# Six more early places for weight chunks of a mixture of experts, and the last norm's vectors loaded late

## The chip, the cores and the metric

The kernel runs on one core of a Trainium2 chip. The metric is the device time of one execution in microseconds (us); three runs of the kernel before gave a median of 1350.39 us. One further execution was taken with the hardware profiler, and all rows below come from that one.

## The reference

Two transformer layers over 256 tokens of width 1024. Layer 0 is a latent attention with a dense feed-forward part, layer 1 a sparse attention with a mixture of eight experts. Only the end of layer 1 matters here:

```python
x = layer_norm(alpha * x + h, ln_mix_g[i], ln_mix_b[i])
logits = xt @ w_router;  top_val, top_idx = lax.top_k(logits, 2);  wts = softmax(top_val)
h = silu(xb @ w_gate[e]) * (xb @ w_up[e])          # 1024 x 3584 twice, for each of 8 experts
y[token] += (h @ w_down[e]) * weight               # 3584 x 1024
x = layer_norm(alpha * x + y, ln_ffn_g[i], ln_ffn_b[i])
```

The eight experts hold 8 x 3 x 1024 x 3584 numbers of 4 bytes, 352 MB, and each is read once.

## The kernel before

**Chunks and places.** The expert weights come from HBM in chunks of 1 MB (some of 0.75 MB), each loaded by SP into a *place*, a tile of 128 x 2048 numbers. There are gate chunks, up chunks and down chunks; this text writes mg(e, j, i), mu(e, j, i) and md(e, j, i) for chunk i of step j of the expert that is worked on as number e. Expert 0 has three steps (512, 2048 and 1024 columns of the 3584), the others two (2048 and 1536). While PE multiplies the gate and up chunks of one step, the down chunks of the step before are put in between: mg, half of md, mu, the other half of md.

**Two kinds of expert.** Experts 0, 2, 4, 6 and 7 are `PLAIN`: PE multiplies the raw chunk as f32 (line 1631), and the place is free when PE has read it. Experts 1, 3 and 5 are split: ACT writes a high part (line 128) and DVE the rest (line 131) into halves `whi` and `wlo` of a ring, and the place is free when both halves are split. The ring has five pairs of halves; one pair is given away as a place (`ring_n`, `given`), which leaves four.

**The order of places** is written by hand (lines 416 to 419): a list `first` for the 18 chunks that are loaded by calls of `pre` while the dense first step of expert 0 runs, then a list `then` that is gone through over and over. A chunk may be loaded as soon as the chunk that had its place before it has been used (`add`, `fetch`, `loads`; `used` calls `loads`). SP issues loads strictly in order, so a load that waits for its place holds those behind it.

```python
first = [["four"] * 2] * 4 + ["hh"] + ["raw"] * 5 + ["xe", "xTh", "xTl", "xna", "xe", "s2", "x3Tl", ["whi", "wlo"]]
then = ["raw"] * 5 + ["xTh", "xTl", "xna", "s2", "x3Tl", ["whi", "wlo"]]
seq = first + then * 2 + (then + ["x3Th"]) * 30
```

With `x3Th` the list has 12 places, so a chunk takes the place of the chunk that came 12 before it. The same four chunks of step 0 of expert 0 are loaded into `four` tiles and split as well.

**Other tiles.** `y` (line 1601) collects the sums of the experts; `scale` (line 1419) starts it as ALPHA times the normed x, two ACT instructions in the dense step. `lng` holds gain and bias of a norm, copied to all 128 partitions by `bc_load` (line 450), two loads on POOL's queue; the last norm's pair is loaded at line 1594, some 850 us before it is used. In `run` (line 1733) the list `fq` holds small thunks; `fill(1)` after each down chunk and `fill(2)` after each gate or up chunk run the next ones.

Of the kernel before, what the change touches and what calls it, by code (L numbers as in the profile page):

```python
# [26 lines left out]
def body(tc, a, out, tap=None, upto=9):  # L27
# [33 lines left out]
    def slot(pool_, tag, bufs=1):  # L61
        return lambda: pool_.tile([128, 2048], F32, tag=tag, bufs=bufs, name=nm("raw"))
# [50 lines left out]
    def ring_half(z, n, dt=F32R):  # L113
        return st.tile([128, 1024], dt, tag=f"{z}{n}", bufs=1, name=nm(z))
# [48 lines left out]
    places = {"raw": s_raw, "four": lambda: four()}  # L163
    for z in ("xna", "xnb", "lng", "xTh", "xTl"):
        places[z] = slot(xp, z)
    for z in ("hh", "s2", "x3Th", "x3Tl"):
        places[z] = lambda z=z: slot(ep, z)()
    places["xe"] = slot(xo, "xe", 2)
    for z in ("whi", "wlo"):
        places[z] = lambda z=z: ring_half(z, given[0], F32)  # L170

    def add(key, src, shape, uses, own=None, auto=True, where="raw", plain=False):

# [27 lines left out]
    def pump(n=1, later=False):  # L201

        for _ in range(n):
            if not halves:
                return
            c, i = halves[0]
            if c.raw is None or c.blocked or c.n > cur[0] + 5 and c.key[0][0] == "m" and len(c.key) > 3:
                return
            if c.own is None:
                if not free:  # L210
                    if ring[0][0].uses[ring[0][1]] > 0:
                        return
                    free.append(ring.popleft()[2])
                    if len(free) + len(ring) > ring_n[0]:
                        given.append(free.pop())
                        continue
                n_ = free.popleft()
                ring.append((c, i, n_))
            elif i == 0:
                c.own = c.own()  # L220
            halves.popleft()

            def done(c=c, i=i):
                c.whole[i] = True
                loads()
            c.parts[i] = split_half(c.raw, i, c.own, later, done, None if c.own else n_)
# [33 lines left out]
            return tuple(t[:, k % (na // 2), c0:nb if c1 is None else c1] for t in c.parts[i])  # L260
        return w

    ring_n, given = [HL], []
    auto = [True]

    def mm3(o, l, r, first, last):
# [146 lines left out]
        yield from (("md", *prev, i) for i in range(wd // 256 - 2))  # L413
        yield from (("md", *prev, i, "tail") for i in range(2))

    first = [["four"] * 2] * 4 + ["hh"] + ["raw"] * 5 + ["xe", "xTh", "xTl", "xna", "xe", "s2", "x3Tl", ["whi", "wlo"]]
    then = ["raw"] * 5 + ["xTh", "xTl", "xna", "s2", "x3Tl", ["whi", "wlo"]]
    keys = list(moe_keys())
    seq = first + then * 2 + (then + ["x3Th"]) * 30
    for n, key in enumerate(keys):  # L420
        where = seq[n]
        if n == len(keys) - 1 and not isinstance(where, list):
# [27 lines left out]
    def bc_load(g, b, p=None, tag="lng"):  # L450

        t = (p or xp).tile([128, 2, D], F32, tag=tag, bufs=1, name=nm("lng"))
        pool.dma_start(t[:, 0, :], g.partition_broadcast(128))
        pool.dma_start(t[:, 1, :], b.partition_broadcast(128))
        return t[:, 0, :], t[:, 1, :]
# [22 lines left out]
    def ln_sums():  # L478
        return xp.tile([128, 16], F32, tag="lnst", bufs=2, name=nm("lnst"))
# [848 lines left out]
    def pre(*ns):  # L1328
        for n in ns:
            fetch(chunks[keys[n]])  # L1330
# [85 lines left out]
        dve.reciprocal(cs[:, 1], cs[:, 0])  # L1416
        dve.tensor_tensor(coef, coef, cs[:, 1, :, None].to_broadcast([128, 2, 8]), op=ALU.mult)

    def scale(t):
        act.activation(y[:, t, :], x3[:, t, :], AF.Copy, scale=ALPHA)  # L1420

    cnt = choice[:, 4]
    pool.tensor_copy(choice[:, 5], iota[:, 0:8])
    ordered = ep.tile([128, 6, 8], F32, name="ordered")
# [161 lines left out]
    transpose_x(x3, x3T, 1, 0)  # L1586
    transpose_x(x3, x3T, 1, 1)
    pump(1)
    pre(13, 14)
    g_ln, b_ln = bc_load(a["ln_ffn_g"][1], a["ln_ffn_b"][1])  # L1590
    dense_u(0, 0)
    logits()
    dense_g(1, 0)
    y = ep.tile([128, 2, D], F32, tag="y", name="y")
    pre(15)
    pump(1)
    logits_T()
    choose()
    dense_g(1, 1)
    pump(1)  # L1600
    slots()
    weigh()
    G0, th = gather(0, 0)
    th[0]()
    dense_u(0, 1)
    scale(0)
    hidden(0)
    scale(1)
    dense_u(1, 0)
    pump(1)  # L1610
    dense_u(1, 1)
    hidden(1)
    pre(16)
    now(th[1:5])
    pump(1)
    hT0 = hid_G(G0)
    flush()
    while ring:
        c, i, n_ = ring.popleft()
        assert c.uses[i] == 0  # L1620
        free.append(n_)
    ring_n[0] -= 1
    given.append(free.pop())
    th[5]()
    pre(17)
    loads()
    auto[0] = True

# [42 lines left out]
    def hidden_tile():  # L1671
        return ep.tile([128, 2048], F32, tag="hh", bufs=1, name=nm("hh"))
# [49 lines left out]
    def scatter(e, oo, ohT, hf, t, sums=None):  # L1722
        c = slice(hf * 512, hf * 512 + 512)
        p = pT()
        pe.matmul(p, ohT[:, t, :], oo[hf][0], start=True, stop=False)
        pe.matmul(p, ohT[:, t, :], oo[hf][1], start=False, stop=True)
        dve.scalar_tensor_tensor(y[:, t, c], p, by[0][:, 2 + t, e:e + 1], y[:, t, c], op0=ALU.mult, op1=ALU.add,
                                 accum_out=sums[t][:, hf:hf + 1] if sums is not None else None)

    def run(todo, G, at, gen=(), end=None):  # L1730


        nxt, acc = None, None
        for n, (e, base) in enumerate(todo):
            ss = widths(e, gen)
            for j, (c0, wd) in enumerate(ss):
                if at is not None and at[:2] == (e, j):
                    continue
                last_j = j == len(ss) - 1
                final = last_j and n == len(todo) - 1  # L1740
                if last_j and not final:
                    nxt, th = gather(*todo[n + 1])
                    th[0]()
                g = gate_up("mg", e, j, G, gen)
                fill(99)
                if len(order) == 1:
                    arrange()
                hh = hidden_tile()
                for z, p in each_bank(hh, g):
                    act.activation(z, p, AF.Silu)  # L1750
                m = 0
                if at is not None:
                    if at[1] == 0:
                        acc = [pB(), pB()]
                    at = (*at[:4], acc, gen)
                    m = widths(at[0], gen)[at[1]][1] // 256
                    down(at, range((m + 1) // 2))
                if last_j and not final:
                    fq.extend(th[1:])
                u = gate_up("mu", e, j, G, gen)  # L1760
                fill(99)
                for z, p in each_bank(hh, u):
                    dve.tensor_tensor(z, z, p, op=ALU.mult)  # L1763
                hT, ths = hid_T(hh, wd, G["plain"])
                if final:
                    now(ths[:0])
                    down(at, range((m + 1) // 2, (m + 1) // 2 + 1))
                    now(ths)
                    down(at, range((m + 1) // 2 + 1, m))
                else:  # L1770
                    down(at, range((m + 1) // 2, m)) if at is not None else None
                    if at is not None and at[0] != e:
                        scatters(at)
                    fq.extend(ths)
                at = (e, j, G, hT)
            if nxt is not None:
                G = nxt
        at = (*at, acc, gen)
        m = wd // 256
        if end is not None:  # L1780
            down(at, range(m - 2))
            oo = []
            end(lambda hf: down_tail(at, hf), lambda hf: oo.append(outs(acc, hf)),
                lambda hf, t, sums: scatter(e, oo, G["ohT"], hf, t, sums))
            return
        down(at, range(m))
        scatters(at)
        fill(99)
# [4 lines left out]
        fq.extend([lambda hf=hf, t=t: scatter(e, oo, G["ohT"], hf, t) for hf in range(2) for t in range(2)])  # L1793

    sums = [ln_sums() for _ in range(2)]

    def n_square(t, hf, scr):
        ln_square(sums[t], y[:, t, :], hf, scr)

    def n_gain(t, hf, z):  # L1800
        ln_gain(sums[t], y[:, t, :], z[:, t, :], g_ln, hf)

    def n_out(t, hf, z):
        ln_out(sums[t], z[:, t, :], b_ln, hf)
        sp.dma_start(out[0, t * 128:(t + 1) * 128, H[hf]], z[:, t, H[hf]])

    def norm_rest(z):
# [32 lines left out]
    assert not halves and not fq and all(c.uses == [0, 0] for c in plan)  # L1840
    man.close()
    free.clear()
    free.extend(z for z in range(HL) if z not in given)
    over = nc.values_load(ordi[0:1, 16:17], min_val=0, max_val=256)  # L1844
    with tc.If(over > 0):
        for e in range(E):
            count = nc.values_load(ordi[0:1, e:e + 1], min_val=0, max_val=256)
            for base in (64, 192) if e in PLAIN else (128,):
                with tc.If(count > base):
                    G, th = gather(e, base, True)  # L1850
                    now(th)
                    run([(e, base)], G, None, ("gen",))
        scr, z = norm_tiles()
        for t in range(2):
            for hf in range(2):
                dve.tensor_reduce(sums[t][:, hf:hf + 1], y[:, t, H[hf]], axis=AX.X, op=ALU.add)
                n_square(t, hf, scr)
        ln_mean(sums[0])
        n_gain(0, 0, z)
        norm_rest(z)  # L1860
# [66 lines left out]
```

## Time and profile before

| | |
|---|---|
| median of three runs | 1350.39 us (1349.46 to 1351.86) |
| the profiled execution, its time | 1349.32 us |
| the profiled execution, its span | 1347.5 us |
| PE busy | 1300.5 us, 97% of the span |
| DVE, ACT, POOL busy | 729.6, 597.3, 42.3 us |
| mean granted TensorE clock | 0.991 |
| DMA | 430.56 MB, of it 421.03 MB on SP's queue |

The span runs from the first to the last instruction; the time is the device time of the whole execution. The page cuts the span into 40 slices and gives for each the busy tenths of every engine, the granted clock and what the DMA engines moved; windows give the same for any stretch. In a timeline a row merges neighbouring equal instructions; a matmul of f32 appears as two records, and a matmul's end in the profile is a model, so its start and the start of the next are the better measure. For DMA issues the last column is the time from issue to landing.

### The profile page before, as it was taken

What the parts mean: (1) busy time and instruction counts of PE and PEld (TensorE: products, weight loads), DVE (VectorE), ACT (ScalarE), POOL (GpSimd) and SP (SyncE); (2) the same over time, 40 slices, a digit from 0 to 9 for tenths busy, and PEclk for the clock granted to TensorE, in tenths of its full rate; (3) what the DMA queues carried; (4) which work ended last, traced back from release to release, by engine and by line L of the source; (5) the groups of instructions that cost most, each with busy time, mean ns of one, the idle gap of its engine ahead of it and who ended that gap; (6) DMA issues with size and microseconds to landing.
All of it is one profiled execution on the core that took longest, in us unless ns stands there. A gap on an engine that the chain in (4) does not pass through costs nothing. (4 is left out here: it accounts for less than half of the span.)

```text
span 1347.5 us, 19685 instructions
## 1 busy us (share of the span) xinstructions
PE 1300.5 (97%) x7397; PEld 925.1 (69%) x7397; DVE 729.6 (54%) x1208; ACT 597.3 (44%) x949; POOL 42.3 (3%) x57
## 2 busy tenths in 40 slices
PE   8998999999999999999999999999999999999884
PEld 7878999989988674367974567894457895543221
DVE  5856555567777761168863257883337875400103
ACT  5554444445577541056752156763126674200001
POOL 0002000002100120000000000000000000000000
PEclk9998999999999999999999999999999999999998
DMA  9635555569622477999999999999999999999994
GB/s 315 211 107 177 165 181 187 188 193 278 197 66 78 146 276 270 410 418 418 417 419 415 418 419 419 416 420 399 418 420 419 416 419 400 418 417 420 418 419 172
DMA packets 127944, 430.56 MB, mean 320 GB/s; under 512 B 12463, under 2 KB 64949, under 8 KB 99808
## 3 DMA queue, kind: packets, MB, share of 16 engines
q1 hardware_dynamic: 125264, 421.03, 80.9%
q0 software_dynamic: 2576, 8.18, 2.1%
q8 instruction: 60, 0.98, 0.3%
q14 instruction: 44, 0.36, 0.1%
HBM read 428.11 MB, written 1.07 MB: 318 GB/s over the span
## 5 line engine op out<-in xcount | busy, mean ns | idle before, releaser
L131 DVE TENSOR_TENSOR wlo<-raw,whi 128x1024 fp32r<-128x1024 f32 (+2 forms) x365 | 413.7, 1152 | 225.2 <-ACT whi L128 216.2
L128 ACT CAST whi<-raw 128x1024 fp32r<-128x1024 f32 (+3 forms) x367 | 360.0, 994 | 255.2 <-PE pa L1631 63.7
L1631 PE MATMUL pa<-raw,xe 128*64 128x512 f32 (+1 forms) x1112 | 238.8, 570 | 6.2 <-DMA raw<-in_moe_w_up_dram 6.2
L1631 PE MATMUL pa<-whi,xe 128*128 128x512 f32 (+3 forms) x820 | 240.2, 382 | 0.0
L1631 PEld LDWEIGHTS pa<-raw,xe 128*64 128x64 f32 x1112 | 74.4, 134 | 146.6 <-issue 119.1
L1631 PEld LDWEIGHTS pa<-whi,xe 128*128 128x128 f32 (+1 forms) x820 | 145.9, 185 | 30.5 <-issue 8.3
L1631 PE MATMUL pa<-wlo,xe 128*128 128x512 f32 (+3 forms) x436 | 153.2, 389 | 0.0
L1631 PE MATMUL pb<-raw,four 128*64 128x512 f32 x520 | 119.0, 596 | 8.4 <-DMA raw<-in_moe_w_down_dram 8.4
L1631 PE MATMUL pb<-whi,four 128*128 128x512 f32 (+1 forms) x356 | 116.5, 408 | 0.0
L1763 DVE TENSOR_TENSOR hh<-hh,pa 128x512 f32<-128x512 f32 (+1 forms) x43 | 25.0, 620 | 145.1 <-PE pa L1631 144.9
L1631 PEld LDWEIGHTS pb<-raw,four 128*64 128x64 f32 x520 | 35.8, 136 | 83.7 <-issue 65.2
L1631 PEld LDWEIGHTS pa<-wlo,xe 128*128 128x128 f32 (+1 forms) x436 | 75.9, 182 | 15.2 <-issue 5.2
L1631 PEld LDWEIGHTS pb<-whi,four 128*128 128x128 f32 (+1 forms) x356 | 65.8, 185 | 24.4 <-issue 7.6
L1631 PE MATMUL pb<-wlo,four 128*128 128x512 f32 (+1 forms) x188 | 75.2, 418 | 0.0
L269 PE MATMUL pa<-xTh,whi 128*128 128x256 f32 x216 | 67.6, 313 | 0.0
L271 PE MATMUL pa<-xTh,wlo 128*128 128x256 f32 x216 | 61.1, 283 | 0.3 <-DVE wlo L131 0.3
L270 PE MATMUL pa<-xTl,whi 128*128 128x256 f32 x216 | 61.2, 283 | 0.0
L1750 ACT ACTIVATE hh<-pa 128x512 f32<-128x512 f32 (+1 forms) x43 | 21.5, 547 | 73.8 <-PE pa L1631 73.8
L269 PE MATMUL pb<-xTh,whi 128*128 128x256 f32 x176 | 49.9, 284 | 0.0
L270 PE MATMUL pb<-xTl,whi 128*128 128x256 f32 x176 | 49.8, 283 | 0.0
L271 PE MATMUL pb<-xTh,wlo 128*128 128x256 f32 x176 | 49.8, 283 | 0.0
L1537 ACT COPY four<-pt 128x512 f32<-128x512 f32 x10 | 5.8, 584 | 90.8 <-PE pt L1531 90.8
(413 smaller groups left out, 1982.3 us busy)
## 6 DMA issues: line engine op xcount, KB each, us to landing
raw<-in_moe_w_down_dram SPq DMA_DIRECT2D x102, 1024.0 KB, 13.2
raw<-in_moe_w_gate_dram SPq DMA_DIRECT2D x63, 1024.0 KB, 11.4
raw<-in_moe_w_up_dram SPq DMA_DIRECT2D x62, 1024.0 KB, 13.7
raw<-in_moe_w_gate_dram SPq DMA_DIRECT2D x51, 768.0 KB, 13.2
raw<-in_moe_w_up_dram SPq DMA_DIRECT2D x51, 768.0 KB, 11.2
raw<-in_nsa_w_in_dram SPq DMA_DIRECT2D x23, 512.0 KB, 7.2
raw<-in_ffn_w_gate_dram SPq DMA_DIRECT2D x11, 1024.0 KB, 5.4
raw<-in_ffn_w_up_dram SPq DMA_DIRECT2D x11, 1024.0 KB, 5.3
```

The costliest lines, as they stand in the source:

```text
L128: act.copy(hi[:, :h], src)
L131: (pool if later == "pool" else dve).tensor_tensor(lo[:, :h], src, f(hi[:, :h]), op=ALU.subtract)
L269: pe.matmul(o, lh, rh, start=first, stop=False)
L270: pe.matmul(o, lh, rl, start=False, stop=False)
L271: pe.matmul(o, ll, rh, start=False, stop=last)
L1537: (dve.tensor_copy if c0 else act.copy)(z, p[:, :n * 128])
L1631: pe.matmul(o, l, r, start=first, stop=last, skip_group_check=True)
L1750: act.activation(z, p, AF.Silu)
L1763: dve.tensor_tensor(z, z, p, op=ALU.mult)
```

## The change

- The four chunks of `first` that were 15 to 17, and six more, get places: `lng`, `s2`, `y`, three pairs of ring halves, `x3Tl`, and two more pairs. So 24 chunks are loaded by `pre` where 18 were, and the load list that follows begins with chunk 24.
- `freed(n)` takes the ring halves of the dense step out of the ring as their last matmul is written, and makes each pair a place. After the dense step one pair stays a place (`R[0]`), and four are the ring, as before.
- `then` gains `lng`, which makes 13 places with `x3Th`. From the first chunk of expert 6 (E - 2) on, `lng` is left out of the list, which makes 12.
- `y` is made and scaled in step 2 of expert 0, behind its gate chunks.
- `bc_load` of the last norm is gone. `gains`, called in step 1 of expert 6 behind its gate chunks, loads gain and bias as 2 x 4 rows of 256 numbers into `few` on SP's queue; four thunks, each two f32 matmuls of 256 columns against a row of the identity and an ACT copy of 512 columns, spread them to 128 partitions.

```diff
-    for z in ("hh", "s2", "x3Th", "x3Tl"):
+    for z in ("hh", "y", "s2", "x3Th", "x3Tl"):
...
-        places[z] = lambda z=z: ring_half(z, given[0], F32)
+        for i in range(HL):
+            places[f"{z}{i}"] = lambda z=z, i=i: ring_half(z, rings[i], F32)
...
-    first = [["four"] * 2] * 4 + ["hh"] + ["raw"] * 5 + ["xe", "xTh", "xTl", "xna", "xe", "s2", "x3Tl", ["whi", "wlo"]]
-    then = ["raw"] * 5 + ["xTh", "xTl", "xna", "s2", "x3Tl", ["whi", "wlo"]]
+    R = [[f"whi{i}", f"wlo{i}"] for i in range(HL)]
+    first = [["four"] * 2] * 4 + ["hh"] + ["raw"] * 5 + ["xe", "xTh", "xTl", "xna", "xe", "lng", "s2", "y", *R[:3], "x3Tl", *R[3:]]
+    then = ["raw"] * 5 + ["xTh", "xTl", "xna", "lng", "s2", R[0], "x3Tl"]
     keys = list(moe_keys())
-    seq = first + then * 2 + (then + ["x3Th"]) * 30
+    seq = first + then + (then + ["x3Th"]) * 30
+
+    n = keys.index(("mg", E - 2, 0, 0))
+    seq[n:] = [z for z in seq[n:] if z != "lng"]
...
-    pre(13, 14)
-    g_ln, b_ln = bc_load(a["ln_ffn_g"][1], a["ln_ffn_b"][1])
+    pre(13, 14, 15)
     dense_u(0, 0)
     logits()
     dense_g(1, 0)
-    y = ep.tile([128, 2, D], F32, tag="y", name="y")
-    pre(15)
+    pre(16, 17)
...
+    def freed(n):
+        for _ in range(n):
+            c, i, n_ = ring.popleft()
+            assert c.uses[i] == 0
+            rings.append(n_)
+
+    freed(1)
+    pre(18)
     slots()
     weigh()
     G0, th = gather(0, 0)
     th[0]()
     dense_u(0, 1)
-    scale(0)
     hidden(0)
-    scale(1)
     dense_u(1, 0)
-    pump(1)
+    freed(2)
+    pre(19, 20)
     dense_u(1, 1)
     hidden(1)
-    pre(16)
+    freed(2)
+    pre(21, 22, 23)
...
+                elif (e, j, gen) == (0, 2, ()):
+                    y = ep.tile([128, 2, D], F32, tag="y", name="y")
+                    ys.append(y)
+                    for t in range(2):
+                        scale(y, t)
+                elif (e, j, gen) == (E - 2, 1, ()):
+                    gains()
...
+    def gains():
+
+        few = xp.tile([128, 512], F32, tag="lnsc", bufs=1, name="few")
+        for i, z in enumerate((a["ln_ffn_g"][1], a["ln_ffn_b"][1])):
+            sp.dma_start(few[4 * i:4 * i + 4, 0:256], z.rearrange("(r n) -> r n", r=4))
+        z = xp.tile([128, 2, D], F32, tag="lng", bufs=1, name=nm("lng"))
+        lng.extend((z[:, 0, :], z[:, 1, :]))
+        zf = z.rearrange("p a b -> p (a b)")
+
+        def go(c):
+            p = pT()
+            for r in (2 * c, 2 * c + 1):
+                pe.matmul(p[:, (r % 2) * 256:(r % 2) * 256 + 256], ident[:8, r:r + 1].to_broadcast([8, 128]), few[:8, 0:256],
+                          start=True, stop=True)
+            act.copy(zf[:, c * 512:(c + 1) * 512], p)
+        fq.extend([lambda c=c: go(c) for c in range(4)])
```

**On SP, as expert 0 begins.** Before, from the first of the chunks loaded last by hand (`mu(0, 1, 0)` and on) to the read of the experts' order:

```order
L91 DMA raw_5273<-in_moe_w_up_dram 128x2048
L91 DMA raw_5275<-in_moe_w_up_dram 128x2048
L91 DMA raw_5323<-in_moe_w_up_dram 128x2048
L84 DMA wlo_5468<-in_moe_w_up_dram 128x1024
L91 DMA raw_5422<-in_moe_w_up_dram 128x2048
L84 DMA whi_5467<-in_moe_w_up_dram 128x1024
L91 DMA raw_5483<-in_moe_w_up_dram 128x2048
```

The same place now:

```order
L91 DMA raw_5273<-in_moe_w_up_dram 128x2048
L91 DMA raw_5275<-in_moe_w_up_dram 128x2048
L91 DMA raw_5277<-in_moe_w_up_dram 128x2048
L91 DMA raw_5321<-in_moe_w_up_dram 128x2048
L91 DMA raw_5323<-in_moe_w_up_dram 128x2048
L84 DMA whi_5354<-in_moe_w_up_dram 128x1024
L84 DMA wlo_5355<-in_moe_w_up_dram 128x1024
L84 DMA whi_5406<-in_moe_w_up_dram 128x1024
L84 DMA wlo_5407<-in_moe_w_up_dram 128x1024
L84 DMA whi_5410<-in_moe_w_up_dram 128x1024
L84 DMA wlo_5411<-in_moe_w_up_dram 128x1024
L91 DMA raw_5432<-in_moe_w_down_dram 128x2048
```

`raw_5483` before and the chunk behind four further `whi` and `wlo` rows now are the first that wait for PE to use up a chunk of expert 0; six chunks more stand ahead of it.

**On SP, in step 1 of expert 6**, the last up chunk of the step (`raw_10293`, mu(6, 1, 7)) and what stands behind it now:

```order
L91 DMA raw_10293<-in_moe_w_up_dram 128x1536
L1816 DMA few<-in_ln_ffn_g_dram 4x256
L1816 DMA few<-in_ln_ffn_b_dram 4x256
L91 ISA
L91 DMA raw_10308<-in_moe_w_down_dram 128x2048
```

The two rows of line 1816 are new; the others stood in this order before.

**On PE, at the same place in the program**, the down chunks md(6, 0, 0) to md(6, 0, 3) and the first up chunk before:

```order
L1631 MATMUL pb_10297<-raw_10148,four_10256 64x512 x2
L1631 MATMUL pb_10298<-raw_10148,four_10256 64x512 x2
L1631 MATMUL pb_10297<-raw_10150,four_10256 64x512 x2
L1631 MATMUL pb_10298<-raw_10150,four_10256 64x512 x2
L1631 MATMUL pb_10297<-raw_10152,four_10256 64x512 x2
```

And now:

```order
L1637 MATMUL pb_10302<-raw_10149,four_10255 64x512 x2
L1637 MATMUL pb_10303<-raw_10149,four_10255 64x512 x2
L1824 MATMUL pt_10310<-few,consts 128x256 x2
L1637 MATMUL pb_10302<-raw_10151,four_10255 64x512 x2
L1637 MATMUL pb_10303<-raw_10151,four_10255 64x512 x2
L1824 MATMUL pt_10320<-few,consts 128x256 x2
L1637 MATMUL pb_10302<-raw_10153,four_10255 64x512 x2
```

A pair of matmuls that reads `few` stands behind each of the four down chunks; the first pair comes one down chunk after the gate chunks of the step.

## Rows read from the trace of the kernel before

**Rows 1.** The page, part 2, two of its lines, slices of 33.7 us.

```profile
DMA  9635555569622477999999999999999999999994
GB/s 315 211 107 177 165 181 187 188 193 278 197 66 78 146 276 270 410 418 418 417 419 415 418 419 419 416 420 399 418 420 419 416 419 400 418 417 420 418 419 172
```

**Rows 2.** Windows of 10 us as expert 0 begins: busy us (instructions), clock, DMA.

```profile
core 0: us, PE busy (x) PEld busy (x) DVE busy (x) ACT busy (x) POOL busy (x), PEclk, DMA share, GB/s
490.00:500.00 10.00, 10.00 (x53) 7.84 (x52) 4.44 (x13) 1.72 (x4) 0.36 (x1) 1.00 0.62 215
500.00:510.00 10.00, 10.00 (x50) 8.28 (x49) 3.92 (x12) 5.97 (x8) 0.00 (x0) 1.00 0.11 47
510.00:520.00 10.00, 10.00 (x71) 7.02 (x71) 3.99 (x13) 2.01 (x5) 0.00 (x0) 1.00 0.56 212
520.00:530.00 10.00, 10.00 (x46) 3.10 (x44) 0.00 (x0) 0.50 (x1) 0.00 (x0) 1.00 0.93 345
```

**Rows 3.** Waits of PE, 1230 to 1330 us: total, times, longest (515 to 1230: none).

```profile
PE pb L1631 <- DMA raw<-in_moe_w_down_dram: 8.4, 15, 1.0
PE pa L1631 <- DMA raw<-in_moe_w_up_dram: 6.2, 13, 1.2
```

**Rows 4.** Windows at expert 6 and near the end, columns as in rows 2.

```profile
1130.00:1140.00 10.00, 10.00 (x47) 3.28 (x48) 5.32 (x5) 4.37 (x5) 0.00 (x0) 1.00 0.99 367
1310.00:1320.00 10.00, 7.75 (x32) 2.03 (x32) 0.00 (x0) 0.00 (x0) 0.00 (x0) 1.00 1.01 417
```

**Rows 5.** Timeline of PE, second gate chunk of expert 6: start us, us, instruction, count.

```profile
1127.38 2.02 PE L1631 MATMUL pa<-raw,xe 128*64 128x512 f32 x8
```

**Rows 6.** Timeline of SP, loads of the up chunks of expert 6.

```profile
1129.43 10.16 SPq L91 DMA_DIRECT2D raw<-in_moe_w_up_dram  x6
```

**Rows 7.** DMA issues, 1129 to 1130 us: count, KB, us from issue to landing.

```profile
raw<-in_moe_w_up_dram SPq DMA_DIRECT2D x1, 1024.0 KB, 5.1
```

**Rows 8.** Tile y: duration ns min/median/max, first and last start us.

```profile
L1420 ACT ACTIVATE y<-x x2: 1056/1056/1057, 501.0 to 505.9; 128x1024 f32<-128x1024 f32 x2
```

**Rows 9.** Window of the second step of expert 0, columns as in rows 2.

```profile
550.00:560.00 10.00, 10.00 (x52) 3.82 (x52) 0.69 (x1) 1.18 (x2) 0.00 (x0) 1.00 1.02 417
```

**Rows 10.** DMA issues, 484 to 500 us.

```profile
lng<-in_ln_ffn_g_dram POOLq DMA_DIRECT2D x1, 512.0 KB, 5.7
```

**Rows 11.** DMA issues, 1187 to 1188 us.

```profile
raw<-in_moe_w_up_dram SPq DMA_DIRECT2D x1, 768.0 KB, 8.8
```

**Rows 12.** DMA issues, first 5 us of the program.

```profile
raw<-in_mla_w_q_up_dram SPq DMA_DIRECT2D x1, 256.0 KB, 11.5
consts<-in_consts_dram SPq DMA_DIRECT2D x1, 64.0 KB, 1.9
```

**Rows 13.** Timeline of PE, expert 6: four down chunks; end of the third up chunk.

```profile
1187.32 7.04 PE L1631 MATMUL pb<-raw,four 128*64 128x512 f32 x32
...
1201.73 0.84 PE L1631 MATMUL pa<-wlo,xe 128*64 128x384 f32 x4
```

**Rows 14.** Timeline of PE, two matmuls of 128x256 f32, two records each.

```profile
51.16 1.13 PE L718 MATMUL pb<-kn,qn 128*128 128x256 f32 x4
```

**Rows 15.** Timeline of PE around its wait at 474 us.

```profile
473.82 0.40 PE L271 MATMUL pa<-whi,xe 128*128 128x512 f32 x1
477.27 0.97 PE L469 MATMUL pt<-consts,x 128*128 128x128 f32 x4 [3.06 <-DVE x L503]
...
478.47 0.63 PE L270 MATMUL pa<-wlo,xe 128*128 128x512 f32 x1
...
481.41 0.39 PE L270 MATMUL pa<-wlo,xe 128*128 128x512 f32 x1
```

**Rows 16.** Window of that wait (after POOL: PEclk, the granted clock).

```profile
470.00:480.00 10.00, 6.94 (x28) 5.41 (x27) 8.85 (x15) 3.41 (x7) 3.51 (x3) 0.87 1.00 385
```

**Rows 17.** Timeline of SP, second half of a load of expert 7.

```profile
1202.61 0.33 SPq L84 DMA_DIRECT2D wlo<-in_moe_w_gate_dram  x1
```

**Rows 18.** DMA issues, 1202.2 to 1203 us.

```profile
wlo<-in_moe_w_gate_dram SPq DMA_DIRECT2D x1, 512.0 KB, 11.4
```

More of the change, by code (lines that the diff above doesn't have):

```diff
@@ L165, in body @@
         places[z] = slot(xp, z)
-    for z in ("hh", "s2", "x3Th", "x3Tl"):
+    for z in ("hh", "y", "s2", "x3Th", "x3Tl"):
         places[z] = lambda z=z: slot(ep, z)()
     places["xe"] = slot(xo, "xe", 2)
+    rings = []
     for z in ("whi", "wlo"):
-        places[z] = lambda z=z: ring_half(z, given[0], F32)
+        for i in range(HL):
+            places[f"{z}{i}"] = lambda z=z, i=i: ring_half(z, rings[i], F32)
     def add(key, src, shape, uses, own=None, auto=True, where="raw", plain=False):
@@ L213, in pump @@
                     free.append(ring.popleft()[2])
-                    if len(free) + len(ring) > ring_n[0]:
-                        given.append(free.pop())
-                        continue
                 n_ = free.popleft()
@@ L261, in get @@
         return w
-    ring_n, given = [HL], []
     auto = [True]
@@ L1417, in weigh, with scale @@
         dve.tensor_tensor(coef, coef, cs[:, 1, :, None].to_broadcast([128, 2, 8]), op=ALU.mult)
-    def scale(t):
+    def scale(y, t):
         act.activation(y[:, t, :], x3[:, t, :], AF.Copy, scale=ALPHA)
+    ys = []
     cnt = choice[:, 4]
@@ L1617, in body @@
     flush()
[L1618 to L1623, printed above, removed]
+    assert not ring and not free
+    free.extend(rings[1:])
     th[5]()
-    pre(17)
     loads()
@@ L1726, in scatter @@
         pe.matmul(p, ohT[:, t, :], oo[hf][1], start=False, stop=True)
+        y = ys[0]
         dve.scalar_tensor_tensor(y[:, t, c], p, by[0][:, 2 + t, e:e + 1], y[:, t, c], op0=ALU.mult, op1=ALU.add,
@@ L1795, in body @@
     sums = [ln_sums() for _ in range(2)]
+    lng = []
+    def gains():
[12 more added lines that the diff above has]
+        fq.extend([lambda c=c: go(c) for c in range(4)])
     def n_square(t, hf, scr):
-        ln_square(sums[t], y[:, t, :], hf, scr)
+        ln_square(sums[t], ys[0][:, t, :], hf, scr)
     def n_gain(t, hf, z):
-        ln_gain(sums[t], y[:, t, :], z[:, t, :], g_ln, hf)
+        ln_gain(sums[t], ys[0][:, t, :], z[:, t, :], lng[0], hf)
     def n_out(t, hf, z):
-        ln_out(sums[t], z[:, t, :], b_ln, hf)
+        ln_out(sums[t], z[:, t, :], lng[1], hf)
         sp.dma_start(out[0, t * 128:(t + 1) * 128, H[hf]], z[:, t, H[hf]])
@@ L1842, in body @@
     free.clear()
-    free.extend(z for z in range(HL) if z not in given)
+    free.extend(rings[1:])
     over = nc.values_load(ordi[0:1, 16:17], min_val=0, max_val=256)
@@ L1855, in body @@
             for hf in range(2):
-                dve.tensor_reduce(sums[t][:, hf:hf + 1], y[:, t, H[hf]], axis=AX.X, op=ALU.add)
+                dve.tensor_reduce(sums[t][:, hf:hf + 1], ys[0][:, t, H[hf]], axis=AX.X, op=ALU.add)
                 n_square(t, hf, scr)
```

## The prediction, on record before the result

> **What bounds the kernel now.** I read the page's slices first. From about 570 us on the DMA engines are full in every slice and move 418 to 420 GB/s, with two dips, 399 and 400 [rows 1]. At 419 GB/s a chunk of 1 MB (1,048,576 bytes) takes 2.50 us. Before that there is room, most of all as expert 0 begins: the windows from 490 to 530 us show DMA shares of 0.62, 0.11, 0.56 and 0.93 while PE is busy for all of each 10 us [rows 2]. The idle parts add up to 3.8 + 8.9 + 4.4 + 0.7 = 17.8 us.
>
> Full DMA engines do not yet make them the bound. So I next read the waits of PE: from 515 to 1230 us there are none, and from 1230 to 1330 us PE waits for raw chunks, 8.4 us for down chunks and 6.2 us for up chunks, 14.6 us together [rows 3]. PE is therefore the bound up to about 1230 us and the loads after it; near the end PE is busy for 7.75 us of 10 while DMA's share is 1.01 [rows 4]. The end comes when the last chunk has landed and the work behind it is done. A change that lets the last chunk land earlier gains, up to 14.6 us; one that makes it land later loses in full; one that merely moves loads within the stretch where PE does not wait gives nothing.
>
> What sets when the last chunk lands? Where the DMA engines are full, the loads ahead of it; where they are not, the release of a place. The second happens once late in the program. The window from 1130 to 1140 us moves only 367 GB/s [rows 4]. There PE ends the second gate chunk of expert 6, mg(6, 0, 1), at 1127.38 + 2.02 = 1129.40 us [rows 5]; SP issues the load into its place 0.03 us later, the first of six up chunks that are spaced over 10.16 us by PE's releases [rows 6]; and it lands 5.1 us after its issue [rows 7], though later ones take 8.8 us [rows 11]. At this point the stream has no lead over the releases: it stands waiting for PE, and begins anew from there.
>
> **The six early places.** Six chunks at 2.50 us are 15.0 us of DMA time, and the 17.8 us of idle time take them. So from 530 us on every load stands up to 15 us earlier than before. None of this shortens PE's work, which does not wait there. Does the lead last to the end? It lives only as long as places are free: a load that comes earlier finds its place still unread and waits on SP. The list has 13 places now up to expert 5, which keeps one chunk more ahead, but from mg(6, 0, 0) on `lng` is out of it and there are 12, as before. So mu(6, 0, 2) takes the place of mg(6, 0, 1) in both kernels; PE, which never waited, ends that chunk at the same 1129.40 us, and the load goes out at the same 1129.43 us. I cost the early loads at **0**: what they win is spent as waiting of SP for places, at the latest at 1129 us, where before had no slack either. Between the ends 0 and -14.6 us I take 0, since rows 5 to 7 show the release as the very thing that the load waited for.
>
> **Work that is moved or dropped, all at 0.** The two ACT instructions that scale `y` take 1.06 us each [rows 8]; they go to the second half of expert 0's work, where ACT is busy for 1.18 of 10 us and PE for all of it [rows 9]; without that cover they would cost 2.1 us. The broadcast of the norm's vectors leaves POOL's queue, two loads of 512 KB with 5.7 us each in a stretch with free DMA time [rows 10]. SP has more issues ahead of its read of the experts' order; that read comes only with the order itself, and SP issues a load in some 0.3 us [rows 17].
>
> **The late vectors: the term that decides.** `gains` issues two small loads on SP's queue, right behind the load of mu(6, 1, 7), at about 1187.9 us. That load needs 8.8 us to land [rows 11], so about 1196.4 us, because 1 MB chunks stand ahead of it. How long does a small one take behind it? Two rows bound that: in the first 5 us 64 KB on an empty queue land after 1.9 us, while 256 KB behind larger loads on SP's queue take 11.5 us [rows 12]. I take the second, the same queue in the same condition: the vectors land with mu(6, 1, 7), at **1196.4 us**.
>
> PE comes to the first pair of matmuls on `few` after one down chunk. The four down chunks start at 1187.32 us and take 7.04 us [rows 13], 1.76 us each, so PE is there at 1189.1 us and waits 1196.4 - 1189.1 = **7.3 us**. All of PE's work stands behind this wait, the three other down chunks and the up chunks, and with it the releases of their places. DMA goes on meanwhile with the loads already issued.
>
> The four thunks themselves: two f32 matmuls of 256 columns took 1.13 us [rows 14]; by the pitch of the down chunks (7.04 / 32 = 0.22 us for 512 columns in a record) four records of 256 would be 0.44 us. I take 0.9, nearer to the row of the same shape: 3.6 us for four, bounds 1.8 and 4.5. A wait of this length also lowers the clock. Behind a wait of 3.06 us a matmul of 512 columns takes 0.63 us where it took 0.40, and 0.39 again by 481.41 us [rows 15], and the granted clock of that window is 0.87 [rows 16]. From 477.27 to 481.41 us are 4.1 us, at most half of them lost; I take 1.8 us, bounds 0 and 3.6.
>
> PE's work behind `gains` is thus late by 7.3 + 3.6 + 1.8 = **12.7 us**. What does that hold up? mu(6, 1, 2) ended at 1201.73 + 0.84 = 1202.57 us [rows 13]; its place takes mg(7, 0, 2), whose second half SP issued at 1202.61 us [rows 17] and which landed 11.4 us later [rows 18], at 1214.0 us. It waited in the queue: with an empty queue 5.1 us would do [rows 7]. So this chunk can be released 11.4 - 5.1 = 6.3 us later at no cost, and it has the least such room of those behind the wait. Late by 12.7 us it is released at 1215.3 us and lands at 1220.4 us, 6.4 us later than before, and every load behind it as well. PE has 14.6 us of waits to give up before the end, so its own 12.7 us vanish there; the DMA's 6.4 us do not.
>
> **Sum.** 0 + 0 + 6.4 us. The profiled execution took 1349.32 us, which gives 1355.7; it lies 1.07 us under the median of the runs, so by the median 1350.39 + 6.4 = **1356.8 us**. With every bound at its low end the shift is 7.3 + 1.8 = 9.1 us and the loss 2.8 us; at the high end 15.4 and 9.1 us: 1353.2 to 1359.5.
>
> **A rule against this.** The row says that a small load behind big ones shares their wait [rows 12]. The Trainium skill, "DMA: Bandwidth & Descriptors", section "Anatomy of one DMA", fits a load's time, on the GpSimd path, as some 2.0 us and its bytes at 436 GB/s, without what is queued ahead. By that the vectors would land about 2 us after their issue, the first rival below; the 11.5 us of rows 12 speak against using it on a full queue, where 256 KB would be 2.6 us.
>
> **Rivals.**
> - *The small loads land at once* (four rows of 1 KB each may pass the chunks if the engines that carry them have little ahead). As the 1.9 us of rows 12, they land at 1189.8 us; PE waits 0.7 us and is late by 0.7 + 3.6 = 4.3 us, less than the 6.3 us of room. No change: **1350.4 us**. With the thunks' 3.6 us, 6.3 - 3.6 = 2.7 us of wait are free, so this holds for landings before 1189.1 + 2.7 = 1191.8 us. For it speaks that the rows of 256 KB in rows 12 are another shape; against it, that all of these loads are on one queue. Chance 0.18.
> - *The lead lasts, faster.* If the loads of expert 6 go out ahead of 1129 us, by a place that comes free earlier than I worked out, the stream after 1130 us has no gap, and up to 14.6 us of PE's waits at the end go: 1350.4 - 14.6 = **1335.8 us**, less by what the vectors take back. It decides from the moment that mu(6, 0, 2) issues before 1129.4 us. Against it: PE's end of mg(6, 0, 1) and the issue lie 0.03 us apart [rows 5, 6]. Chance 0.08.
> - *The change doesn't do what it says*: the six loads land no earlier, as SP is held by an early wait. The end does not change by it, so it has no price of its own and stands with the forecast.
>
> **How the numbers follow.** The forecast has 0.74, the rivals 0.18 and 0.08. A measurement of this kernel tells about 0.2%, 2.7 us, from no change. The forecast's own range, 1353.2 to 1359.5, lies wholly above that, so slower is 0.74, within 0.2% is 0.18, faster 0.08. The range takes in the first rival, down to the lowest run of before (1349.5), and at the top the upper bound with half a microsecond for the spread of the runs: 1349.4 to 1360.0. The faster rival stays out.
>
> **What would show it.** Right: the windows from 490 to 530 us are nearly full; from some place in experts 1 to 5 on, loads are issued at PE's releases; the load of mu(6, 0, 2) is issued at 1129.4 us as before; the two rows of line 1816 take 8 to 9 us to land; PE shows one wait for `few` of about 7 us near 1189 us, with a granted clock under 1 behind it; a gap in the DMA share at about 1200 to 1215 us; the waits for raw chunks after 1230 us shrink by about 6 us. Wrong: the vectors land in 2 us (then no change), or the loads of expert 6 run ahead of PE's releases and PE's waits at the end shrink while the end comes earlier.

## The result

| | median of four runs | lowest to highest |
|---|---|---|
| before | 1349.93 us | 1348.56 to 1351.86 |
| with the change | 1361.82 us | 1359.80 to 1363.36 |

The ratio is 1.009, with a 95% interval of 1.0072 to 1.0108: the change costs 11.9 us. The forecast was slower, by 6.4 us, to 1356.8 us with a range up to 1360.0. The sign was right, and the size lies outside the range. The four runs with the change stand in two pairs: 1359.80 and 1360.33 us at a mean granted clock of 0.988, 1363.30 and 1363.36 us at 0.986 and 0.984. The profiled execution is the lowest of them, with a span of 1357.7 us; it took 10.5 us more than the profiled execution of the kernel before (1359.80 and 1349.32 us).

The ratios below compare the runs of an experiment with runs of the kernel before in the same series, and can differ from the quotient of the two medians. Two of the six executions of e8, the profiled one among them, took 2601 and 3212 us and are not in its ratio.

**The profile after, where the early loads are.** The windows of [rows 2], in the changed kernel, same columns:

```profile
490.00:500.00 10.00, 10.00 (x56) 7.83 (x54) 3.66 (x11) 1.71 (x4) 0.00 (x0) 1.00 0.64 222
500.00:510.00 10.00, 10.00 (x53) 8.42 (x53) 4.43 (x13) 3.29 (x5) 0.00 (x0) 1.00 0.92 342
510.00:520.00 10.00, 10.00 (x68) 6.44 (x69) 3.48 (x13) 2.01 (x5) 0.00 (x0) 1.00 1.00 393
520.00:530.00 10.00, 10.00 (x48) 3.20 (x46) 0.00 (x0) 0.97 (x2) 0.00 (x0) 1.00 0.94 349
```

DMA shares of 0.11 and 0.56 have become 0.92 and 1.00: the six chunks are loaded there. The landing time of the same chunk in the two traces (us from the start of the span) shows how long the lead lasts:

```
chunk            lands before   lands after   earlier by
mg(0, 2, 2)          541.2         526.2         15.0
mu(0, 2, 2)          562.4         547.0         15.5
mg(1, 1, 2)          631.2         618.9         12.3
mu(1, 1, 6)          663.9         653.7         10.2
md(1, 1, 2)          703.2         697.6          5.5
mg(2, 1, 0)          732.9         730.4          2.4
mg(6, 0, 0)         1102.0        1098.7          3.3
mu(6, 0, 3)         1137.0        1136.5          0.6
mu(6, 1, 0)         1183.1        1182.6          0.5
```

PE itself is 0.6 us earlier here in this execution, so a lead of 0.5 us is none. The last of it goes where the prediction said. mu(6, 0, 2) goes into a pair of ring halves now, and its two halves are issued at 1127.97 and 1128.87 us, each 0.04 us after PE has read the half that was there. In the changed kernel the windows at the start of expert 6 show DMA with nothing to do for a fifth of the time, as it waits for places:

```profile
1120.00:1130.00 10.00, 10.00 (x49) 5.53 (x49) 2.80 (x4) 1.52 (x3) 0.00 (x0) 1.00 0.78 292
1130.00:1140.00 10.00, 10.00 (x48) 3.11 (x44) 5.32 (x5) 4.31 (x6) 0.00 (x0) 1.00 1.00 361
```

**The profile after, where the time goes.** Waits of PE from 515 us to the end (total, times, longest):

```profile
PE pb L1637 <- DMA raw<-in_moe_w_down_dram: 8.2, 14, 1.0
PE pt L1824 <- DMA few<-in_ln_ffn_b_dram: 7.1, 1, 7.1
PE pa L1637 <- DMA raw<-in_moe_w_up_dram: 2.5, 6, 0.9
```

The second line is new: one wait of 7.1 us for the last norm's vectors. The two others are the waits of [rows 3], 14.6 us there and 10.7 us now, 3.9 us less where the prediction had some 6. (e1 below, which loses nothing, has 10.6 us, so this figure does not tell of the loss.) The view of the tile `few` has the two loads, issued at 1187.3 and 1187.7 us:

```profile
L1816 SPq DMA_DIRECT2D few<-in_ln_ffn_g_dram x1: 380/380/380, 1187.3 to 1187.3; - x1
L1816 SPq DMA_DIRECT2D few<-in_ln_ffn_b_dram x1: 262/262/262, 1187.7 to 1187.7; - x1
```

And the timeline of PE behind them, which answers to [rows 13]:

```profile
1186.68 1.88 PE L1637 MATMUL pb<-raw,four 128*64 128x512 f32 x8
1195.70 2.04 PE L1824 MATMUL pt<-few,consts 8*128 8x256 f32 x4 [7.14 <-DMA few<-in_ln_ffn_b_dram]
1197.67 3.68 PE L1637 MATMUL pb<-raw,four 128*64 128x512 f32 x8
1201.29 2.07 PE L1824 MATMUL pt<-few,consts 8*128 8x256 f32 x4
1203.29 3.59 PE L1637 MATMUL pb<-raw,four 128*64 128x512 f32 x8
1206.81 1.12 PE L1824 MATMUL pt<-few,consts 8*128 8x256 f32 x4
1207.87 1.94 PE L1637 MATMUL pb<-raw,four 128*64 128x512 f32 x8
...
1217.65 1.57 PE L1637 MATMUL pa<-raw,xe 128*64 128x384 f32 x8
```

The last line is mu(6, 1, 2). 4 KB took 8.0 us from the second issue to PE's start. Behind the wait two thunks and two down chunks take about twice their time (2.04 for 1.12, 3.68 for 1.94): the granted clock is at its lower level of 1.2 GHz, and it comes back at about 1206.7 us, 11 us after PE began again. The windows (columns as above; the last two are of 2 us) show that, and what it does to the loads:

```profile
1190.00:1200.00 10.00, 4.30 (x10) 1.93 (x12) 0.00 (x0) 0.58 (x1) 0.00 (x0) 0.65 0.68 280
1200.00:1210.00 10.00, 10.00 (x29) 3.35 (x26) 0.00 (x0) 1.17 (x2) 0.00 (x0) 0.67 0.51 168
1210.00:1220.00 10.00, 10.00 (x66) 6.04 (x67) 0.00 (x0) 1.70 (x4) 0.00 (x0) 1.00 0.97 356
...
1204.00:1206.00 2.00, 2.00 (x8) 0.47 (x4) 0.00 (x0) 0.00 (x0) 0.00 (x0) 0.50 0.80 332
1206.00:1208.00 2.00, 2.00 (x10) 0.80 (x8) 0.00 (x0) 0.03 (x1) 0.00 (x0) 0.84 0.24 37
```

The kernel before, in the first two of these windows:

```profile
1190.00:1200.00 10.00, 10.00 (x62) 5.12 (x59) 0.00 (x0) 0.37 (x1) 0.00 (x0) 1.00 1.02 419
1200.00:1210.00 10.00, 10.00 (x62) 4.72 (x63) 0.58 (x2) 0.75 (x2) 0.00 (x0) 1.00 1.01 418
```

DMA moves 280 and 168 GB/s in 20 us where the kernel before moved 419 and 418, since no place comes free. From mg(7, 0, 5) on the chunks land 11.4 to 11.5 us later than before, up to the last one (1339.2 us for 1327.8). The span grows by 10.2 us only: behind DVE's last instruction it has 6.9 us more to its end before (1340.6 to 1347.5) and 5.7 us now (1352.0 to 1357.7). What makes these 1.2 us, no run here shows.

### The profile page after: what moved, and what is told of

It is laid out like the page before. It is cut to its first block, busy times and chain, and to the rows that moved or that the text cites. A ratio compares the mean times of both kernels' runs of the same rounds, so it can differ in the third digit from the quotient of the medians.

```text
span 1357.7 us, 19707 instructions
## 1 busy us (share of the span) xinstructions
PE 1307.8 (96%) x7413; PEld 927.9 (68%) x7413; DVE 730.3 (54%) x1208; ACT 600.3 (44%) x953; POOL 41.1 (3%) x55
## 3 DMA queue, kind: packets, MB, share of 16 engines
q0 software_dynamic: 2288, 7.14, 1.7%
## 5 line engine op out<-in xcount | busy, mean ns | idle before, releaser
L131 DVE TENSOR_TENSOR wlo<-raw,whi 128x1024 fp32r<-128x1024 f32 (+2 forms) x379 | 431.1, 1156 | 224.3 <-ACT whi L128 216.1
L128 ACT CAST whi<-raw 128x1024 fp32r<-128x1024 f32 (+3 forms) x381 | 375.5, 997 | 257.3 <-PE pa L1637 84.4
L1637 PE MATMUL pa<-whi,xe 128*128 128x512 f32 (+3 forms) x848 | 247.6, 389 | 0.0
L1637 PE MATMUL pa<-raw,xe 128*64 128x512 f32 (+1 forms) x1056 | 225.4, 568 | 2.5 <-DMA raw<-in_moe_w_up_dram 2.5
L1637 PEld LDWEIGHTS pa<-raw,xe 128*64 128x64 f32 x1056 | 70.8, 134 | 133.9 <-issue 119.0
L1637 PE MATMUL pa<-wlo,xe 128*128 128x512 f32 (+3 forms) x464 | 160.5, 402 | 0.0
L1637 PE MATMUL pb<-whi,four 128*128 128x512 f32 (+1 forms) x364 | 120.4, 412 | 0.2 <-DMA whi<-in_moe_w_down_dram 0.2
L1637 PE MATMUL pb<-wlo,four 128*128 128x512 f32 (+1 forms) x196 | 79.0, 425 | 0.0
## 6 DMA issues: line engine op xcount, KB each, us to landing
raw<-in_moe_w_down_dram SPq DMA_DIRECT2D x104, 1024.0 KB, 11.4
```

The source lines that it names most:

```text
L128: act.copy(hi[:, :h], src)
L131: (pool if later == "pool" else dve).tensor_tensor(lo[:, :h], src, f(hi[:, :h]), op=ALU.subtract)
L1637: pe.matmul(o, l, r, start=first, stop=last, skip_group_check=True)
```

## The experiments

To compare single executions, the loss is read below as the time from the start of md(6, 0, 0) to the landing of the last chunk: 140.5 us before, 152.5 us with the change, 12.0 us more. In the same way PE's lateness is read at the end of mu(6, 1, 2): 15.2 us behind that start before, 32.5 us with the change, 17.3 us late.

**e1: the same, with the vectors asked for one step earlier.**

```diff
-                elif (e, j, gen) == (E - 2, 1, ()):
-                    gains()
+                elif (e, j, gen) == (E - 2, 0, ()):
+                    few_load()
+                elif (e, j, gen) == (E - 2, 1, ()):
+                    gains()
```

> The changed kernel with the two small loads issued one step earlier (as step 0 of expert 6 begins), the four thunks where they are. Theory (the loss comes from PE's wait for the vectors, its clock behind it, and the places released late): no wait for few, no fall of the clock, PE late by the four thunks alone, some 4.2 us, less than the 5 to 6 us that the releases have to spare; the time is that of the kernel before, 1350 us within 2. Rival (the longer list of early places, or the thunks themselves, cost part of it): 1353 us or more although the wait is gone.

Measured: 1349.05 us, ratio to before 0.9995 (0.9984 to 1.0006). The timeline of PE:

```profile
1190.19 1.88 PE L1637 MATMUL pb<-raw,four 128*64 128x512 f32 x8
1192.00 1.12 PE L1833 MATMUL pt<-few,consts 8*128 8x256 f32 x4
1193.05 1.94 PE L1637 MATMUL pb<-raw,four 128*64 128x512 f32 x8
1194.92 1.13 PE L1833 MATMUL pt<-few,consts 8*128 8x256 f32 x4
1195.97 1.94 PE L1637 MATMUL pb<-raw,four 128*64 128x512 f32 x8
```

There is no wait and no fall of the clock; from start to start a thunk takes 1.05 us and the chunk behind it 1.87. PE is 4.8 us late at mu(6, 1, 2), and the last chunk is not late (140.1 us). As the forecast had it, all of the loss, to within the 0.8 us that the interval leaves, is the wait and what follows from it; the thunks fit in the room that the releases have.

**e3: the early places alone**, vectors early by POOL as before, `lng` not a place.

```diff
     pre(13, 14, 15)
+    g_ln, b_ln = bc_load(a["ln_ffn_g"][1], a["ln_ffn_b"][1])
...
-                elif (e, j, gen) == (E - 2, 1, ()):
-                    gains()
```

> The changed kernel with the vectors loaded early by POOL as before, so without gains, and with five early places instead of six (lng holds the vectors, and the list has 12 places throughout). Theory (the lead of the early loads is lost at the releases of experts 2 to 6): 1350 us within 1.5, first loads of expert 0's later steps 12 to 13 us earlier than before, loads of expert 6 less than 1 us earlier. Rival 1 (part of the lead lasts): 1347 us or less. Rival 2 (the early places cost something that the late vectors hide): 1353 us or more.

Measured: 1348.58 us, 0.9991 (0.9981 to 1.0001). Five early places without the late vectors gain 1.2 us at the middle of the interval, and nothing that can be told from no change. The loads of expert 0's last step land 11 to 13 us earlier (mg(0, 2, 2) 11.2), those of expert 6 no earlier, and the last chunk lands 140.5 us behind md(6, 0, 0), as before. The forecast holds.

**e4 and e8: the late vectors alone**, put into the kernel before. In e4 nothing held the two loads back, and they stood at 496 us in SP's queue, far ahead of their place. So e4 measured something else than it was made for; e8 holds them (lines against e4, shortened):

```diff
+        act.copy(few[:8, 0:1], late[:8, 0:1])
         for i, z in enumerate((a["ln_ffn_g"][1], a["ln_ffn_b"][1])):
             sp.dma_start(few[4 * i:4 * i + 4, 0:256], z.rearrange("(r n) -> r n", r=4))
```

> The kernel before with one part of the change, the last norm's vectors loaded late and spread by the four thunks; its places are as before. Theory (the whole loss is here): 1360 to 1363 us, a wait for few of about 7 us, 11 to 12 us lost. Rival (the loss needs the longer list, whose drop from 13 to 12 places comes near): 1355 us or less.

Measured: 1348.09 us, 0.9992 (0.9981 to 1.0002), with no wait: a second case, beside e1, of the thunks at their place at no cost. It decides nothing between theory and rival.

> The kernel before with the vectors loaded late, as in e4, but held at the place where the change has them: an ACT copy of 8 numbers from the last gate sums of the step into few goes ahead of the two loads, so that they cannot be issued before about 1187.5 us. Theory (the whole loss is the wait for the vectors and what follows it): a wait for few of about 7 us, a granted clock of about 0.65 behind it, 1359 to 1363 us. Rival (the loss needs the longer list of places): 1355 us or less with the same wait.

Measured: 1.0071 (1.0054 to 1.0088), which is 9.6 us, by four executions from 1357.89 to 1365.08 us. One more execution gave the profile:

> The kernel of e8 once more, for a profile of an undisturbed execution. Theory: one wait for few of about 7 us, half-level clock behind it, the loads of expert 7 later by 9 to 12 us, counted from the first down chunk of the step. Rival: a shorter wait or later loads by less than 6 us.

Measured: 1359.07 us. The timeline of PE:

```profile
1187.23 1.89 PE L1630 MATMUL pb<-raw,four 128*64 128x512 f32 x8
1197.90 2.04 PE L1813 MATMUL pt<-few,consts 8*128 8x256 f32 x4 [8.77 <-DMA few<-in_ln_ffn_b_dram]
1199.87 3.68 PE L1630 MATMUL pb<-raw,four 128*64 128x512 f32 x8
```

The wait is 8.8 us where about 7 was expected, PE is 16.7 us late and the last chunk 10.7 us. The loss is there without any of the new places, so the longer list and its drop from 13 to 12 places are not needed for it.

**e2 and e9: another queue.** In e2 the two loads are on POOL's queue (`pool.dma_start`); they too went out early, at 489 us. e9 holds them with the same ACT copy.

> The changed kernel with the two small loads on POOL's queue at the same place in the program. Theory (they are late because SP's queue keeps its order): they land in 2 to 4 us, PE waits 1 to 3 us, the end is late by 0 to 3 us: 1350 to 1353 us. Rival (the DMA engines are full, whatever the queue): they land 7 to 9 us after their issue, and the time is that of the changed kernel, 1360 to 1363 us.

Measured: 1349.91 us, 0.9996 (0.9986 to 1.0006), without a wait, for the reason given: again a case like e1.

> The changed kernel with the two small loads on POOL's queue, held by the same copy so that they are issued at about 1187.7 us and not at 489 us as in e2. Theory (SP's queue keeps its order, another queue does not stand behind it): they land 2 to 5 us after their issue, PE waits 1 to 4 us, 1350 to 1356 us. Rival (the DMA engines serve what came first whatever the queue): they land 7 to 9 us after issue and the time is 1360 to 1363 us.

Measured: 1358.45 us, 1.0062 (1.0045 to 1.0079); neither expectation. The DMA issues of e9 from 1190.5 to 1192 us (count, KB, us to landing):

```profile
raw<-in_moe_w_up_dram SPq DMA_DIRECT2D x1, 768.0 KB, 9.8
few<-in_ln_ffn_g_dram POOLq DMA_DIRECT2D x1, 4.0 KB, 4.8
few<-in_ln_ffn_b_dram POOLq DMA_DIRECT2D x1, 4.0 KB, 4.8
```

Of POOL's queue (q0) no packet ran from 1192.0 to 1194.5 us; from 1194.5 to 1196.0 us (packets, MB, share of 16 engines):

```profile
q1 hardware_dynamic: 110, 0.60, 98.8%
q0 software_dynamic: 64, 0.01, 3.6%
```

On POOL's queue the vectors land 4.8 us after issue, with the DMA engines full, and over 3 us of that pass before their first packet; in e2 at 489 us, with DMA's share at 0.99 from 488 to 494 us, it was 4.9 and 4.7 us. So POOL's queue does not stand behind all of SP's chunks, where the chunk issued beside them took 9.8 us, but it is no matter of 2 us either. The Trainium skill, "DMA: Bandwidth & Descriptors", section "Queues, rings and completion order", has each DMA engine take turns between the queues it has work for, and consume one queue's descriptors in order; the 4.8 us on POOL's queue and the 8.0 us on SP's agree with that. PE waited 4.3 us and was 12.2 us late, and the last chunk 7.1 us:

```profile
1196.32 2.04 PE L1825 MATMUL pt<-few,consts 8*128 8x256 f32 x4 [4.32 <-DMA few<-in_ln_ffn_b_dram]
```

**e5 and e6: which part of the clock's cost is whose.** e5 puts two empty entries ahead of the four thunks; e6 leaves the first thunk and puts the others behind the gather.

```diff
-        fq.extend([lambda c=c: go(c) for c in range(4)])
+        fq.extend([lambda: None] * 2 + [lambda c=c: go(c) for c in range(4)])
```

> The changed kernel with the four thunks two down chunks later; loads as in the change. PE's wait is then about 7.1 - 2 x 1.8 = 3.5 us. Theory 1 (the clock stays low for as long as it did in the change, about 11 us after the wait, whatever the wait's length): PE late by 3.5 + 4.2 + 5.5 = 13 us, 1357 to 1359 us. Theory 2 (a shorter wait costs less clock, as the wait of 3.06 us at 474 us did): PE late by 3.5 + 4.2 + 2 = 10 us, 1353 to 1356 us. Rival (the end does not go by how late PE is at these chunks): 1361 us.

Measured: 1356.74 us, 1.0042 (1.0022 to 1.0062), between the ranges of the two theories. The rival's 1361 us is not met. The timeline of PE:

```profile
1198.69 1.89 PE L1824 MATMUL pt<-few,consts 8*128 8x256 f32 x4 [3.31 <-DMA few<-in_ln_ffn_b_dram]
1200.51 3.68 PE L1637 MATMUL pb<-raw,four 128*64 128x512 f32 x8
```

The wait is 3.3 us, and the profiled execution then has the lower clock to 1209.1 us (read from windows of 2 us, as in the other cases below), 10 us after PE began again. But the nine runs of this one program differ: 1351.15, 1351.18 and 1351.32 us at a mean granted clock of 0.990 to 0.992 over the execution, 1354.46 at 0.989, 1356.74 to 1356.94 at 0.986 to 0.987, 1360.43 and 1360.51 at 0.984. The same program costs between 2 and 11 us over the kernel before, and its time goes with the clock. So its median cannot choose between the theories, and one execution shows one case of several.

```diff
-        fq.extend([lambda c=c: go(c) for c in range(4)])
+        fq.extend([lambda: go(0)] + [lambda: None] * 3)
+        later.extend([lambda c=c: go(c) for c in range(1, 4)])
```

> The changed kernel with only the first thunk at its place; the other three stand behind the gather of the next expert's tokens, among the up chunks. The wait stays at 7.1 us; behind it PE now has down chunks for raw weights and no matmuls of 8 rows. Theory 1 (the long stretch at half clock comes from the length of the wait): it lasts about 11 us again, 1358 to 1361 us. Theory 2 (it comes from the four thunks, whose matmuls use 8 rows of the array, put between the down chunks): it ends some 4 us after the wait, 1354 to 1357 us.

Measured: 1358.20 us, 1.0060 (1.0044 to 1.0077), in the range of theory 1. The timeline of PE:

```profile
1199.17 2.04 PE L1826 MATMUL pt<-few,consts 8*128 8x256 f32 x4 [7.13 <-DMA few<-in_ln_ffn_b_dram]
1201.14 7.92 PE L1637 MATMUL pb<-raw,four 128*64 128x512 f32 x24
```

The lower clock lasts to 1206.3 us, 7.1 us of PE's work, with down chunks alone behind the first thunk: longer than theory 2 has it without the thunks, shorter than the 11 us of theory 1. The time alone would have spoken for theory 1, but the moved thunks add lateness of their own (below). Behind the same wait of 7.1 us the change has 11 us; e5 has 10 us behind 3.3 us of wait, e9 6.4 us behind 4.3, e8 6.3 us behind 8.8. So the length of the wait does not set it in these executions, and the matmuls of 8 rows are not needed for it. Neither theory holds as it stands; with one execution of each, and e5 so different from run to run, what does set it stays open.

**e10: the releases late without a wait.** As e1, each thunk does its work twice.

```diff
-        fq.extend([lambda c=c: go(c) for c in range(4)])
+        fq.extend([lambda c=c: (go(c), go(c)) for c in range(4)])
```

> As e1 (small loads early, no wait), but each of the four thunks does its work twice: two more matmul pairs and ACT copies of the same numbers at each place. PE is late by about 9.5 us at mu(6, 1, 2) with no wait and the clock at its full level. Theory (the end goes by how late the places of expert 6 come free, less about 5 us to spare, whatever made them late): 1353 to 1355 us. Rival (the loss needs the wait or the fall of the clock as such): 1351 us or less.

Measured: 1353.03 us, 1.0018 (1.0008 to 1.0028), in the range of the theory. The timeline of PE shows the doubled thunks, at the full clock:

```profile
1191.89 1.99 PE L1833 MATMUL pt<-few,consts 8*128 8x256 f32 x8
1193.81 1.94 PE L1637 MATMUL pb<-raw,four 128*64 128x512 f32 x8
```

PE is 8.3 us late, by work alone, and the last chunk 3.1 us. Lateness beyond 5 to 6 us reaches the last chunk, whatever made it:

```
             PE late at mu(6, 1, 2)   last chunk late   difference
e1                    4.8                 -0.4             5.2
e10                   8.3                  3.1             5.2
e9                   12.2                  7.1             5.1
e8, again            16.7                 10.7             6.0
the change           17.3                 12.0             5.3
```

e5 and e6 do not belong in the rows, since PE's matmuls stand in another order there and the chunks behind mu(6, 1, 2) are late by more. In e5 PE is 10.6 us late at mu(6, 1, 2) and 12.1 at mu(6, 1, 3), and the last chunk is 5.9 us late; in e6, with its three moved thunks, it is 11.9 and 12.9, and the last chunk 8.7 us.

**e7: `lng` longer in the list, the vectors later.** `lng` stays in the list to the middle of expert 7; the loads of the vectors go out in step 0 of expert 7 and the thunks run in its step 1.

```diff
-    n = keys.index(("mg", E - 2, 0, 0))
+    n = keys.index(("mg", E - 1, 1, 0))
...
-                elif (e, j, gen) == (E - 2, 1, ()):
-                    gains()
+                elif (e, j, gen) == (E - 1, 0, ()):
+                    few_load()
+                elif (e, j, gen) == (E - 1, 1, ()):
+                    gains()
```

> A version meant to beat both: as the change, but lng stays in the list of places until mg(7, 1, 0), so there are 13 places through expert 6 and half of expert 7; the two small loads are issued in step 0 of expert 7 and the four thunks run in its step 1, where PE waits for loads anyway. Theory (the lead of the early loads is lost where the list has too few places, by the releases of expert 6): the loads of expert 6 come one release earlier, some 2 to 3 us, all the later ones too, and the time is 1346 to 1348 us, 2 to 3 us below the kernel before. Rival (the lead is lost again behind expert 6, or the thunks at the end show): 1349 us or more.

Measured: 1348.24 us against 1349.80 in the same series, 0.9981 (0.9972 to 0.9990). The medians are 1.6 us apart, the ratio makes it 2.6 us (1.3 to 3.8): a small gain, clear of no change, with the median just above the forecast's range and below the rival's. The windows at the start of expert 6, and PE's waits from 1230 to 1330 us:

```profile
1120.00:1130.00 10.00, 10.00 (x48) 5.83 (x46) 3.53 (x4) 1.07 (x2) 0.00 (x0) 1.00 0.99 392
1130.00:1140.00 10.00, 10.00 (x46) 3.27 (x47) 5.32 (x5) 4.37 (x5) 0.00 (x0) 1.00 0.98 369
...
PE pb L1637 <- DMA raw<-in_moe_w_down_dram: 5.8, 10, 0.9
PE pa L1637 <- DMA raw<-in_moe_w_up_dram: 2.5, 6, 0.5
```

292 GB/s have become 392 in the first, and the last chunk lands 137.9 us behind md(6, 0, 0), 2.6 us earlier than before. One place more where the releases bind brings about one chunk's time (2.5 us). PE's waits for raw chunks after 1230 us are 8.3 us here, 14.6 before.

## Why the prediction was wrong in size

**Right: what bounds the kernel, and the early places at 0.** The loads were 15 us ahead, and the lead was gone at mu(6, 0, 2); e1 and e3 give no change for the places. Most of it went sooner than at 1129 us, between the second steps of experts 1 and 2 (12.3 us at mg(1, 1, 2), 2.4 at mg(2, 1, 0)), which the words "at the latest" covered.

**Right: the moved and dropped work at 0.** e1 contains all of it, e3 all but the dropped broadcast, and both measure no change.

**Right: the vectors land with the chunk ahead of them.** Forecast 1196.4 us and a wait of 7.3; measured 1195.7 and 7.14, and mu(6, 1, 7) itself landed at 1196.0. The chunks ahead of it are of 0.75 MB, not of 1 MB as the prediction says; its 8.8 us are read from the row and do not hang on that. The row of 256 KB behind larger loads [rows 12] was the right one to take: 8.0 us on SP's queue are not the 2 us of the rule that the prediction sets against that row.

**Nearly right: the thunks.** 3.6 us were taken. In e1 they make PE 4.8 us late: 4 x 1.05 us, and 0.1 us or so for each change of operation between them and the chunks. The row of the same shape, 1.13 us [rows 14], was nearer than the 0.9 taken.

**Wrong: "A wait of this length also lowers the clock ... I take 1.8 us, bounds 0 and 3.6".** From 1195.70 to 1206.81 us two thunks and two down chunks took 11.1 us; in e1 the same four take 1197.84 - 1192.00 = 5.8 us. The clock cost 5.3 us, beyond the upper bound. What failed is the length of the low stretch: the prediction took the 4.1 us behind one wait elsewhere [rows 15, 16] and lost a little under half of it, and here PE worked at the lower clock for 11 us and again lost about half (in e9 12.2 - 4.3 - 4.8 = 3.1 of 6.4 us). The bound was only the price doubled, with nothing in the trace that limits it. 7.1 + 4.8 + 5.3 = 17.2 us against the 17.3 measured; the forecast had 12.7. Why the stretch was 11 us long here stays open.

**Too large by one: "this chunk can be released 6.3 us later at no cost".** Between the kernels 5.3 us were to spare, 5.1 to 6.0 in the experiments with the same order of PE's work. The 5.1 us from issue to landing is that of a chunk that finds the engines idle. Behind the stall places come free every 1.4 us or so from 1219.3 us on, a chunk of 1 MB takes 2.5 us, and so the loads queue again: mg(7, 0, 3), the one behind mg(7, 0, 2), took 7.2 us from the issue of its first half and was 11.2 us late, and from mg(7, 0, 5) on it is 11.5.

So 17.3 - 5.3 = 12.0 us where 12.7 - 6.3 = 6.4 stood: 4.6 us from lateness (3.5 of them the clock, 1.2 the thunks, the wait 0.2 the other way), 1.0 us from the room. This is the account of one execution's loads. That its 12.0 us meet the 11.9 us between the medians is in part chance: the profiled pair differs by 10.5 us, and the median of the change lies between its two pairs of runs, of which only the lower one has a profile.

Of the rivals, the small loads landing at once is out on SP's queue (8.0 us) and the lasting lead is out for this list; e7 shows that it lasts in part, 2.6 us of 14.6, where the list is not shortened at expert 6.

## What to carry to other kernels

A small load that is needed soon should not be issued on a queue with megabytes in flight: issue it a step earlier (e1: the loss is gone, to within 0.8 us). Where PE is never late, price a new wait of it as wait, work and clock together, and take the clock's part with a wide upper bound. Early loads are worth only what the narrowest later release leaves of them: count the places where the releases bind, and lengthen the list there, not where there is room.

## What was not expected of the hardware

- Waits of PE of 3.3 to 8.8 us were each followed by 6 to 11 us of work at 1.2 GHz, not longer behind the longer waits, and the same program (e5) took from 1351.15 to 1360.51 us in nine runs, in step with its mean granted clock (0.990 to 0.992 in the fastest three, 0.984 in the slowest two).
- 4 KB on POOL's queue took 4.7 to 4.9 us from issue to landing, both times with DMA engines that were full; on SP's queue behind 0.75 MB chunks it took 8.0 us from the second issue to PE's start in the change and in e6, and 9.6 us in the later execution of e8.
